# Where the last query projection and the output projection's first part stand among the attention blocks of a two-layer diffusion transformer

## The chip, the cores and the metric

The kernel runs as one program on one core of a Trainium2 chip. The metric is device time of one execution. TensorE (PE, with its weight loads as PEld), VectorE (DVE), ScalarE (ACT), GpSimd (POOL) and SyncE (SP, which here only issues transfers) each work through their own instructions in a fixed order and wait for each other by semaphores.

## The reference, cut to what matters

The network has 2 layers over two streams of 256 tokens: the latents (stream 0) and the context (stream 1). In the last layer only stream 0 goes on past the keys and values. The part between the two feed-forward halves of a layer is the one that is changed:

```python
px = modulate(rms_norm(h, g_mix[l]), sh2, sc2) @ w_in[l]      # and pc for the context
aq, ak, av, hy, nq, nk, nv = split_proj(px)
qa = axial_rope(rms_norm(to_heads(aq, 8), g_q_attn[l]), cos, sin)     # 8 query heads
ya = gqa_latent(qa, ka, av, kca, vca)      # latents see 256 context + 256 latent keys
yb = hyena_mixer(hy, ...)                  # long convolution
yc = neighbourhood_attention(qn, kn, nv, kcn, vcn, rpb)   # 4 heads, with a bias
h = h + gt2 * (jnp.concatenate([ya, yb, yc], -1) @ w_out[l])
# layer 0 only: the same for the context stream, whose queries see the 256 context keys
```

## The kernel before, in words

All of it is in float32. Each dense product is made of three matmuls on split operands: a weight half tile is split into `whi` (ScalarE, line 337) and `wlo` (VectorE, line 338), the activations into `xh` and `xl`. Four split halves can be held at a time.

`mix` (from line 618) runs once per layer. Tokens stand in four blocks `tt` of 128: blocks 2 and 3 are context (256 keys), 0 and 1 latent (512 keys). In layer 0 the order of the blocks is 2, 3, 0, 1, in layer 1 it is 0, 1. There are three groups `g` of four heads: group 0 is the neighbourhood ("near") heads, groups 1 and 2 are the grouped-query heads.

`project(c, use)` (matmuls on lines 680 to 682) is a generator: each step issues 24 matmuls for one stream and half of the weights; after the last step `use` takes the result out of PSUM. With two streams a projection is 4 steps, 96 matmuls, and holds two of the four PSUM banks named `mm`; in layer 1 it is 2 steps, 48 matmuls, one bank. Projection 4 makes the queries of group 1, projection 5 those of group 2. `heads` (lines 695 to 725) normalises and rotates them, `stack_q` (lines 753 to 768) splits and transposes them (line 763) into `qs`.

`attend(tt, g, fill, steps)` (line 836) does one block and group, head by head: scores into an `mm` bank (line 858 for near heads, 863 and 864 for grouped heads), maximum (line 871 or 875), exponential on ScalarE (873 or 877), reciprocal and scaling (878, 879), transposes on TensorE (882), copy to `pT` on ScalarE (884), and after each second head the product with V (889) into an `aux` bank. Between the heads it draws `steps` steps from the generator `fill`, so that other matmuls stand there. Latent near blocks load a bias tile (line 849) into the one buffer `zt`, which the block before has to have read.

Before the change, `fill` in the near group is projections 4 and 5 in a row, 4 steps per block. The first block of group 1 has no filler; then the results of the convolution and of the near heads are split into `xh`, `xl` (chunks 4 to 7; `split`, lines 895 to 897), the queries of group 2 are stacked (they had been kept as `raw` in the list `late`), and from there on `first_part`, the output projection's tiles 0 and 1 over chunks 4 to 7, is the filler: 32 steps of 3 matmuls each (lines 352 to 354), 3 per block in layer 0, 6 in layer 1. What is left of it runs after the last block. The second part, tiles 2 and 3 over chunks 0 to 3, follows.

The order on each engine is set when the program is built: a scheduler works from the order of the Python code with its own estimates, and moves instructions forward or back past each other.

Of the kernel before, what the change touches and what calls it, by code (L numbers as in the profile page):

```python
# [11 lines left out]
F32 = mybir.dt.float32  # L12
# [6 lines left out]
P = 128  # L19
# [3 lines left out]
NT = 512  # L23
# [18 lines left out]
class Net:  # L42
# [575 lines left out]
    def mix(self, l, streams, after):  # L618
        nc, v = self.nc, self.nc.vector
        ns = len(streams)  # L620
        both = (0, 1)
        n = SEQ * ns
        spec, fnorm = self.spec
        with ExitStack() as es:
            mp = es.enter_context(self.tc.tile_pool(name=f"mix{l}", bufs=1))
# [7 lines left out]
            rq = mp.tile([P, 4, 12], F32, name="rq")  # L633
# [4 lines left out]
            for m in range(3):  # L638
                if m < 2:
                    pts = early[m]  # L640
                else:
                    pts = (self.ps(), self.ps())
# [25 lines left out]
            def project(c, use):  # L668
                live = both if c < 2 or c == 3 else streams
                pts = {s: self.ps() for s in live}  # L670
                for half in range(2):
                    hi, lo = self.next_half(("in", l, c), half)
                    for s in live:
                        for i in range(2):
                            t = slice((2 * s + i) * P, (2 * s + i + 1) * P)
                            out = pts[s][:, i * 256:(i + 1) * 256]
                            for k in range(4):
                                kk = half * 4 + k
                                w = slice(k * 256, (k + 1) * 256)
                                nc.tensor.matmul(out, self.xh[:, kk, t], hi[:, w], start=kk == 0 and i == 0, stop=False)  # L680
                                nc.tensor.matmul(out, self.xh[:, kk, t], lo[:, w], start=False, stop=False)  # L681
                                nc.tensor.matmul(out, self.xl[:, kk, t], hi[:, w], start=False, stop=kk == 7 and i == 1)  # L682
                            yield
                use(pts)

            def run(*parts):
                for part in parts:
                    for _ in part:
                        pass

            def heads(src, nh, s, rope, gain, rdst, put):


                w = nh * DH
                raw = mp.tile([P, 2, w], F32, tag="qraw", name="qraw", bufs=4)
                sq = mp.tile([P, 2, w], F32, tag="sqk", name="sqk", bufs=2)
                nc.scalar.copy(raw, src)
                nc.scalar.activation(sq, raw, AF.Square)
                ss = mp.tile([P, 2 * nh], F32, tag="ss", name="ss", bufs=2)
                v.tensor_reduce(out=ss, in_=sq.rearrange("p t (h d) -> p (t h) d", d=DH), axis=AX.X, op=ALU.add)  # L700
                v.tensor_scalar(out=ss, in0=ss, scalar1=1.0 / DH, scalar2=EPS, op0=ALU.mult, op1=ALU.add)
                r = self.rsqrt(ss, 2 * nh, f"q{nh}")
                if rdst is not None:
                    v.tensor_scalar(out=rdst, in0=r.rearrange("p (t h) -> p t h", t=2), scalar1=-0.5 * QSCALE, scalar2=None,
                                    op0=ALU.mult)
                else:
                    r3 = raw.rearrange("p t (h d) -> p (t h) d", d=DH)
                    v.scalar_tensor_tensor(out=r3, in0=r3, scalar=-0.5,
                                           in1=r.rearrange("p (h o) -> p h o", o=1).to_broadcast([P, 2 * nh, DH]),
                                           op0=ALU.mult, op1=ALU.mult)  # L710
                if rope is not None and s == 0:
                    for i in range(2):
                        s5 = sq[:, i].rearrange("p (h a b e) -> p h a b e", h=nh, a=2, b=2)
                        r5 = raw[:, i].rearrange("p (h a b e) -> p h a b e", h=nh, a=2, b=2)
                        st = tabs[:, rope, i, 1].rearrange("p (o a b e) -> p o a b e", o=1, a=2, b=2)
                        for b in range(2):
                            nc.gpsimd.tensor_tensor(out=s5[:, :, :, b], in0=r5[:, :, :, 1 - b],
                                                    in1=st[:, :, :, b].to_broadcast([P, nh, 2, 16]), op=ALU.mult)
                        rh = raw[:, i].rearrange("p (h d) -> p h d", d=DH)
                        v.tensor_tensor(out=rh, in0=rh, in1=tabs[:, rope, i, 0:1, :].to_broadcast([P, nh, DH]), op=ALU.mult)  # L720
                    v.tensor_tensor(out=raw, in0=raw, in1=sq, op=ALU.add)
                else:
                    r3 = raw.rearrange("p t (h d) -> p (t h) d", d=DH)
                    v.tensor_tensor(out=r3, in0=r3, in1=self.gqk[:, l, gain:gain + 1, :].to_broadcast([P, 2 * nh, DH]), op=ALU.mult)
                put(raw, s)
# [26 lines left out]
            def stack_q(p0):  # L752

                def put(raw, s):
                    for t in range(2):
                        st = mp.tile([P, 4, 2, DH], F32R, tag="qraw", name="qst", bufs=4)
                        r = raw[:, t].rearrange("p (h c) -> p h c", h=4)
                        nc.scalar.copy(st[:, :, 0], r)
                        v.tensor_tensor(out=st[:, :, 1], in0=r, in1=st[:, :, 0].bitcast(F32), op=ALU.subtract)
                        pt = self.ps("aux")  # L760
                        flat = st.rearrange("p h w c -> p (h w c)").bitcast(F32)
                        for i in range(4):
                            nc.tensor.transpose(pt[:, i * P:(i + 1) * P], flat[:, i * P:(i + 1) * P], self.ident)
                        tag, bufs = ("uc", 6) if len(qs) < 4 else ("qs", 4)
                        qs[p0, 2 * s + t] = mp.tile([P, 512], F32R, tag=tag, name="qs", bufs=bufs)
                        self.copy(qs[p0, 2 * s + t], pt)
                return put

            two = lambda pt: pt.rearrange("p (t c) -> p t c", t=2)
# [15 lines left out]
                for s in (1, 0):  # L785
                    nc.scalar.copy(V[:, 2 * s:2 * s + 2, P:], two(pts[s]))

            late = []

            def grouped_q(p0):  # L790
                put = stack_q(p0) if p0 == 0 else lambda raw, s: late.append((raw, s))

                def use(pts):
                    for s in streams[::-1]:
                        heads(two(pts[s]), 4, s, 0, 0, rq[:, 2 * s:2 * s + 2, 2 * p0:2 * p0 + 4], put)
                return use

            run(project(0, grouped_kv))
# [3 lines left out]
            zt = mp.tile([P, 2, 512], F32, tag="zt", name="zt")  # L802
# [92 lines left out]
            def split(c0, n, cols, src):  # L895
                nc.scalar.copy(yh[:, c0:c0 + n, cols], src)
                v.tensor_tensor(out=yl[:, c0:c0 + n, cols], in0=src, in1=yh[:, c0:c0 + n, cols].bitcast(F32), op=ALU.subtract)

            order = [0, 1] if ns == 1 else [2, 3, 0, 1]
            fill = chain(project(4, grouped_q(0)), project(5, grouped_q(2)))  # L900
            near = mp.tile([P, 2, NT], F32, name="near")
            for tt in order:
                yo = attend(tt, 0, fill, 4)
                nc.scalar.copy(near[:, :, tt * P:(tt + 1) * P], yo)
            rest = [(g, tt) for g in (1, 2) for tt in order]
            yo = attend(rest[0][1], 1, fill, 0)
            run(fill)
            yh, yl = self.xh, self.xl
            for cb in range(2):
                split(4 + cb, 1, slice(0, n), yt[cb][:, :n].rearrange("p (o t) -> p o t", o=1))  # L910
            split(6, 2, slice(0, n), near[:, :, :n])


            self.begin_sum()
# [12 lines left out]
                                self.residual(pt, l, 5, 4 * m + 2 * half + i, s, s * SEQ)  # L927

            fill = first_part()
            for g, tt in rest:  # L930
                if (g, tt) != rest[0]:
                    yo = attend(tt, g, fill, 3 if ns == 2 else 6)
                if (g, tt) == rest[0]:
                    for raw, s in late:
                        stack_q(2)(raw, s)
                if (g, tt) == rest[-1]:
                    run(fill)
                split(2 * g - 2, 2, slice(tt * P, (tt + 1) * P), yo)
            units = [(m, half) for m in (2, 3) for half in range(2)]
            if ns == 2:  # L940
                hl = {u: self.next_half(("out", l, u[0]), u[1]) for u in units}
                steps = after()
# [148 lines left out]
```

## Time and profile before

| | us |
|---|---|
| median of 3 runs (1768.14 to 1769.57) | 1768.63 |
| the profiled execution's own time | 1769.55 |
| its span in the trace | 1767.8 |
| TensorE busy | 1726.6 |
| VectorE busy | 1146.6 |
| ScalarE busy | 649.3 |

The changed part is two short stretches of the span: attention blocks and fillers run from about 518 to 640 us in layer 0 and from about 1482 to 1551 us in layer 1. Matmuls overlap in their pipeline, so the duration of a row on PE is longer than the step from one matmul to the next; where a row's start is given beside the next one's, the difference is the step. The same holds, by less, for rows on VectorE and ScalarE.

### The profile page before, as it was taken

How to read it: one execution, taken by the hardware profiler on the slowest of the kernel's cores; microseconds unless marked ns; L12 is line 12 of the kernel's file. 1: busy time of each engine (PE TensorE's matmuls, PEld its weight loads, DVE VectorE, ACT ScalarE, POOL GpSimd, SP SyncE). 2: the span in 40 equal slices, each digit the busy share in tenths (PEclk: the TensorE clock that was granted, in tenths of full speed). 3: DMA queues.
4: the chain of work that ended last, by engine and by line, in shares of the span. 5: the costliest groups of instructions: out<-in, count | busy, mean ns of one | idle time of the engine just before them, and what ended most of it. 6: DMA issues, size and time to landing. Idle time of an engine off the chain costs nothing.

```text
span 1767.8 us, 24967 instructions
## 1 busy us (share of the span) xinstructions
PE 1726.6 (98%) x9996; PEld 1478.5 (84%) x9996; DVE 1146.6 (65%) x2218; ACT 649.3 (37%) x1053; POOL 90.5 (5%) x128
## 2 busy tenths in 40 slices
PE   7999999999999999999999999999999999989999
PEld 3787888889887688888888898888888898789999
DVE  4778778757657868676676475454544587865554
ACT  4422222234337744222222342222222355744443
POOL 0000000011110020000000110000000301010000
PEclk9999999999999999999999999999999999989999
DMA  7765455532211023544543335534432233135553
GB/s 266 294 194 179 178 183 204 181 124 72 96 60 37 25 85 132 172 163 168 164 177 141 110 110 190 172 126 147 160 134 87 93 130 110 49 119 171 182 185 131
DMA packets 47429, 251.95 MB, mean 143 GB/s; under 512 B 5999, under 2 KB 7233, under 8 KB 29521
## 3 DMA queue, kind: packets, MB, share of 16 engines
q1 hardware_dynamic: 47106, 250.26, 40.9%
q8 instruction: 78, 1.28, 0.3%
q14 instruction: 37, 0.30, 0.1%
q0 software_dynamic: 64, 0.10, 0.0%
q10 hardware_dynamic: 144, 0.01, 0.0%
HBM read 249.30 MB, written 1.05 MB: 142 GB/s over the span
## 4 chain that ended last, share of the span: by engine, by line
PE 90%; DVE 6%; ACT 2%; issue 1%; POOL 0%; DMA 0%; DVEq 0%; POOLq 0%; ACTq 0%
PE mm L352 26%; PE mm L353 26%; PE mm L354 25%; PE mm L680 2%; PE mm L682 2%; PE mm L681 2%; PE aux L889 1%; DVE wlo L338 1%; PE aux L882 1%; ACT whi L337 1%; PE aux L613 1%; PE mm L858 1%; PE aux L827 1%; DVE h L447 0%; PE aux L125 0%
## 5 line engine op out<-in xcount | busy, mean ns | idle before, releaser
L352 PE MATMUL mm<-xh,whi 128*128 128x512 f32 (+1 forms) x1760 | 607.7, 349 | 9.0 <-ACT xh L441 3.8
L353 PE MATMUL mm<-xl,whi 128*128 128x512 f32 (+1 forms) x1760 | 609.6, 348 | 3.2 <-DVE xl L442 2.0
L354 PE MATMUL mm<-xh,wlo 128*128 128x512 f32 (+1 forms) x1760 | 608.6, 347 | 0.0
L338 DVE TENSOR_TENSOR wlo<-raw,whi 128x1024 fp32r<-128x1024 f32 x324 | 387.3, 1197 | 233.0 <-ACT whi L337 229.5
L337 ACT CAST whi<-raw 128x1024 fp32r<-128x1024 f32 x324 | 332.3, 1027 | 541.5 <-PE mm L353 353.7
L352 PEld LDWEIGHTS mm<-xh,whi 128*128 128x128 f32 x1760 | 332.1, 190 | 55.5 <-ACT xh L201 6.4
L353 PEld LDWEIGHTS mm<-xl,whi 128*128 128x128 f32 x1760 | 334.4, 190 | 47.0 <-DVE xl L442 2.6
L354 PEld LDWEIGHTS mm<-xh,wlo 128*128 128x128 f32 x1760 | 333.9, 190 | 42.2 <-issue 2.2
L352 PE MATMUL mm<-hh,whi 128*128 128x512 f32 (+1 forms) x788 | 271.2, 344 | 0.0
L353 PE MATMUL mm<-hl,whi 128*128 128x512 f32 (+1 forms) x788 | 271.0, 344 | 0.1
L354 PE MATMUL mm<-hh,wlo 128*128 128x512 f32 (+1 forms) x788 | 270.3, 343 | 0.0
L505 DVE TENSOR_TENSOR gs<-gs,mm 128x512 f32<-128x512 f32 (+1 forms) x88 | 54.5, 621 | 186.1 <-ACT gs L504 147.7
L352 PEld LDWEIGHTS mm<-hh,whi 128*128 128x128 f32 x788 | 149.3, 189 | 19.2 <-issue 1.9
L353 PEld LDWEIGHTS mm<-hl,whi 128*128 128x128 f32 x788 | 149.3, 190 | 18.9 <-issue 1.1
L354 PEld LDWEIGHTS mm<-hh,wlo 128*128 128x128 f32 x788 | 149.3, 189 | 17.4
L447 DVE SCALAR_TENSOR_TENSOR h<-mm,mod,h 128x256 f32<-128x256 f32 x216 | 98.6, 479 | 90.9 <-PE mm L354 90.2
L285 DVE CUSTOM_DVE_ANT_0 ada<-ada,cb 128x1024 f32<-128x1024 f32 x128 | 155.9, 1221 | 2.4 <-DMA ada<-wada 0.4
L504 ACT ACTIVATE gs<-mm 128x512 f32<-128x512 f32 (+1 forms) x88 | 47.8, 544 | 275.6 <-PE mm L354 271.7
L285 DVE CUSTOM_DVE_ANT_0 prod<-ada,cb 128x1024 f32<-128x1024 f32 x96 | 116.9, 1218 | 0.0
L374 POOL TENSOR_TENSOR acc<-acc,sq 128x256 f32<-128x256 f32 x61 | 52.7, 869 | 1234.7 <-ACT sq L370 1195.9
L680 PE MATMUL mm<-whi,xh 128*128 128x256 f32 x336 | 97.4, 290 | 0.0
L681 PE MATMUL mm<-wlo,xh 128*128 128x256 f32 x336 | 96.7, 288 | 0.0
(178 smaller groups left out, 1443.5 us busy)
## 6 DMA issues: line engine op xcount, KB each, us to landing
raw<-wgu SPq DMA_DIRECT2D x86, 1024.0 KB, 4.8
ada<-wada SPq DMA_DIRECT2D x128, 512.0 KB, 3.7
raw<-wd SPq DMA_DIRECT2D x32, 896.0 KB, 4.6
raw<-wd SPq DMA_DIRECT2D x16, 1024.0 KB, 4.9
raw<-win SPq DMA_DIRECT2D x12, 1024.0 KB, 4.8
a<-wada SPq DMA_DIRECT2D x8, 1024.0 KB, 5.2
raw<-wout SPq DMA_DIRECT2D x8, 1024.0 KB, 4.9
raw<-why SPq DMA_DIRECT2D x6, 1024.0 KB, 4.9
```

The costliest lines, as they stand in the source:

```text
L285: nc.vector.tensor_tensor_reduce(out=prod, in0=w, in1=self.cb[:, s], scale=1.0, scalar=0.0, op0=ALU.mult, op1=ALU.add, accum_out=m[:, s, j ...
L337: nc.scalar.copy(hi[:, :n], raw)
L338: nc.vector.tensor_tensor(out=lo[:, :n], in0=raw, in1=hi[:, :n].bitcast(F32), op=ALU.subtract)
L352: t.matmul(out, whi, xhi, start=start, stop=False)
L353: t.matmul(out, whi, xlo, start=False, stop=False)
L354: t.matmul(out, wlo, xhi, start=False, stop=stop)
L374: nc.gpsimd.tensor_tensor(out=self.acc[s], in0=self.acc[s], in1=sq, op=ALU.add)
L447: return self.nc.vector.scalar_tensor_tensor(out=self.h[:, j, cols], in0=ps[:, c0:c0 + SEQ], scalar=self.mod(l, ch, s, j), in1=self.h[:, j ...
L504: nc.scalar.activation(gs[:, :n], pg[:, :n], AF.Silu)
L505: nc.vector.tensor_tensor(out=gs[:, :n], in0=gs[:, :n], in1=pu[:, :n], op=ALU.mult)
L680: nc.tensor.matmul(out, self.xh[:, kk, t], hi[:, w], start=kk == 0 and i == 0, stop=False)
L681: nc.tensor.matmul(out, self.xh[:, kk, t], lo[:, w], start=False, stop=False)
```

## The change

Projection 4 alone is now the filler of the near group, and projection 5 becomes that of group 1. The output of group 1 isn't split block by block: ScalarE copies each block from PSUM into a new buffer `first` (which takes the buffer `zt`), and one split of all blocks follows. `first_part` now stands wholly in group 2. The list `late` is gone: the queries of group 2 are stacked as soon as they are made. In Python the numbers of steps are also set anew.

```diff
             def grouped_q(p0):
-                put = stack_q(p0) if p0 == 0 else lambda raw, s: late.append((raw, s))
-
                 def use(pts):
                     for s in streams[::-1]:
-                        heads(..., rq[:, 2 * s:2 * s + 2, 2 * p0:2 * p0 + 4], put)
+                        heads(..., rq[:, 2 * s:2 * s + 2, 2 * p0:2 * p0 + 4], stack_q(p0))
                 return use
...
-            fill = chain(project(4, grouped_q(0)), project(5, grouped_q(2)))
+            pace = (3, 3, 2, 1) if ns == 2 else (3, 2)
             near = mp.tile([P, 2, NT], F32, name="near")
-            for tt in order:
-                yo = attend(tt, 0, fill, 4)
+            fill = project(4, grouped_q(0))
+            for tt, steps in zip(order, pace):
+                yo = attend(tt, 0, fill, steps)
                 nc.scalar.copy(near[:, :, tt * P:(tt + 1) * P], yo)
-            rest = [(g, tt) for g in (1, 2) for tt in order]
-            yo = attend(rest[0][1], 1, fill, 0)
+            run(fill)
+            fill = project(5, grouped_q(2))
+            first = mp.tile([P, 2, NT], F32, tag="zt", name="first")
+            for tt, steps in zip(order, pace):
+                yo = attend(tt, 1, fill, steps)
+                nc.scalar.copy(first[:, :, tt * P:(tt + 1) * P], yo)
             run(fill)
...
             split(6, 2, slice(0, n), near[:, :, :n])
+            split(0, 2, slice(0, n), first[:, :, :n])
...
             fill = first_part()
-            for g, tt in rest:
-                if (g, tt) != rest[0]:
-                    yo = attend(tt, g, fill, 3 if ns == 2 else 6)
-                if (g, tt) == rest[0]:
-                    for raw, s in late:
-                        stack_q(2)(raw, s)
-                if (g, tt) == rest[-1]:
+            for tt, steps in zip(order, (2, 6, 12, 12) if ns == 2 else (10, 22)):
+                yo = attend(tt, 2, fill, steps)
+                if tt == order[-1]:
                     run(fill)
-                split(2 * g - 2, 2, slice(tt * P, (tt + 1) * P), yo)
+                split(2, 2, slice(tt * P, (tt + 1) * P), yo)
```

First place: TensorE in layer 0, in the last near block (`kT,qT` are near scores, `ident,pr` transposes, `pT,V` products with V, `whi,xh` and its like a projection). Before, its last scores stand among matmuls of projection 5:

```order
L858 MATMUL mm<-kT,qT 128x512
L882 MATMUL aux<-ident,pr 128x128 x4
L681 MATMUL mm<-wlo,xh 128x256
L858 MATMUL mm<-kT,qT 128x512
L682 MATMUL mm<-whi,xl 128x256
L680 MATMUL mm<-whi,xh 128x256
L681 MATMUL mm<-wlo,xh 128x256
```

After, from the block's first score to the first score of group 1 (`khi,qs`), with `ident,qst` as the transposes of group 1's queries:

```order
L682 MATMUL mm<-whi,xl 128x256
L854 MATMUL mm<-kT,qT 128x512
L878 MATMUL aux<-ident,pr 128x128 x8
L854 MATMUL mm<-kT,qT 128x512 x2
L885 MATMUL aux<-pT,V 64x128 x8
L854 MATMUL mm<-kT,qT 128x512
L878 MATMUL aux<-ident,pr 128x128 x8
L885 MATMUL aux<-pT,V 64x128 x8
L878 MATMUL aux<-ident,pr 128x128 x8
L763 MATMUL aux<-ident,qst 128x128 x7
L885 MATMUL aux<-pT,V 64x128 x8
L763 MATMUL aux<-ident,qst 128x128
```

No filler is left between the last near block's first score and group 1's first score.

Second place: TensorE in layer 0, in the last latent block of group 1. Before, matmuls of `first_part` stand among its heads:

```order
L863 MATMUL mm<-khi,qs 128x512
L889 MATMUL aux<-pT,V 64x128 x8
L864 MATMUL mm<-klo,qs 128x512
L352 MATMUL mm<-xh,whi 128x512
L353 MATMUL mm<-xl,whi 128x512
L882 MATMUL aux<-ident,pr 128x128 x4
L354 MATMUL mm<-xh,wlo 128x512
```

After, from the last matmul of projection 5 on:

```order
L682 MATMUL mm<-whi,xl 128x256
L859 MATMUL mm<-khi,qs 128x512
L885 MATMUL aux<-pT,V 64x128 x8
L878 MATMUL aux<-ident,pr 128x128 x8
L860 MATMUL mm<-klo,qs 128x512
L859 MATMUL mm<-khi,qs 128x512
L860 MATMUL mm<-klo,qs 128x512
L859 MATMUL mm<-khi,qs 128x512
L885 MATMUL aux<-pT,V 64x128 x8
L860 MATMUL mm<-klo,qs 128x512
```

The scores of the last head, two batches of transposes, two products with V and the transposes of group 2's queries follow, without a filler, until group 2 begins; the 96 matmuls of `first_part` then stand among group 2's heads, 87 of them before its last score.

## Rows read from the trace of the kernel before

**Rows 1.** The page: span and busy time by engine.
```profile
span 1767.8 us, 24967 instructions
PE 1726.6 (98%) x9996; PEld 1478.5 (84%) x9996; DVE 1146.6 (65%) x2218; ACT 649.3 (37%) x1053; POOL 90.5 (5%) x128
```

**Rows 2.** Windows: stretch, its length, busy time by engine, TensorE clock, DMA.
```profile
518.00:567.00 49.00, 48.54 (x350) 37.21 (x349) 33.59 (x113) 31.71 (x75) 1.91 (x4) 1.00 0.15 55
567.00:601.00 34.00, 29.66 (x219) 21.82 (x217) 28.80 (x105) 25.84 (x64) 2.31 (x4) 0.95 0.10 32
601.00:640.00 39.00, 38.28 (x288) 29.52 (x287) 28.47 (x89) 24.43 (x62) 0.00 (x0) 1.00 0.20 67
1482.00:1507.00 25.00, 23.85 (x177) 18.39 (x177) 20.82 (x58) 19.76 (x40) 1.89 (x4) 1.00 0.29 106
1507.00:1529.00 22.00, 20.09 (x179) 16.23 (x179) 21.14 (x69) 18.58 (x43) 2.01 (x4) 1.00 0.14 50
...
580.00:590.00 10.00, 7.38 (x37) 5.11 (x37) 8.49 (x32) 5.87 (x16) 0.00 (x0) 0.83 0.32 107
660.00:670.00 10.00, 6.98 (x53) 6.32 (x52) 9.49 (x23) 5.62 (x11) 4.46 (x4) 1.00 0.29 105
```

**Rows 3.** Timeline of PE, 566 to 590 us: the rows with idle time before them.
```profile
572.52 0.66 PE L889 MATMUL aux<-pT,V 128*64 128x128 f32 x8 [0.48 <-ACT pT L884]
...
574.95 0.41 PE L882 MATMUL aux<-ident,pr 128*128 128x128 f32 x2 [0.88 <-DVE rst L72]
...
582.93 0.38 PE L863 MATMUL mm<-khi,qs 128*128 128x256 f32 x1 [1.29 <-ACT pr L877]
...
584.34 0.50 PE L863 MATMUL mm<-khi,qs 128*128 128x512 f32 x1 [0.91 <-ACT pr L877]
```

**Rows 4.** Timeline of PE: steps of fillers, near scores, products with V, transposes.
```profile
512.02 0.28 PE L680 MATMUL mm<-whi,xh 128*128 128x256 f32 x1
512.14 0.28 PE L681 MATMUL mm<-wlo,xh 128*128 128x256 f32 x1
...
539.50 1.13 PE L858 MATMUL mm<-kT,qT 64*128 64x512 f32 x4
...
561.21 1.12 PE L858 MATMUL mm<-kT,qT 64*128 64x512 f32 x2
...
562.93 1.09 PE L889 MATMUL aux<-pT,V 128*64 128x128 f32 x16
...
568.26 1.09 PE L882 MATMUL aux<-ident,pr 128*128 128x128 f32 x8
...
637.06 0.39 PE L352 MATMUL mm<-xh,whi 128*128 128x512 f32 x1
637.29 0.39 PE L353 MATMUL mm<-xl,whi 128*128 128x512 f32 x1
```

**Rows 5.** Timeline of DVE in a latent near block.
```profile
541.17 1.22 DVE L338 TENSOR_TENSOR wlo<-raw,whi 128x1024 fp32r<-128x1024 f32 x1 [4.24 <-ACT whi L337]
542.31 0.48 DVE L870 SCALAR_TENSOR_TENSOR pr<-mm,rq,bias 128x256 f32<-128x256 f32 x1
542.71 0.67 DVE L700 TENSOR_REDUCE ss<-sqk 128x8 f32<-128x512 f32 x1
543.30 0.67 DVE L871 TENSOR_REDUCE mx<-pr 128x1 f32<-128x512 f32 x1
...
546.64 0.47 DVE L879 TENSOR_SCALAR pr<-pr,mx 128x512 f32<-128x512 f32 x1
547.04 0.16 DVE L73 TENSOR_SCALAR rsu<-rst 128x8 f32<-128x8 f32 x1
```

**Rows 6.** Groups of ACT by line and shape, 518 to 640 us.
```profile
L884 ACT COPY pT<-aux 128x512 f32<-128x512 f32 x24 | 13.9, 588 | 5.8 <-PE aux L882 5.2
...
L877 ACT ACTIVATE pr<-mm,mx,rq 128x512 f32<-128x512 f32 x16 | 12.4, 781 | 2.4 <-DVE mx L876 2.4
```

**Rows 7.** The bias tile: its landing time.
```profile
DMA to landing us min/median/max: 3.3/3.4/3.6
```

More of the change, by code (lines that the diff above doesn't have):

```diff
@@ L786, in near_v @@
                     nc.scalar.copy(V[:, 2 * s:2 * s + 2, P:], two(pts[s]))
-            late = []
             def grouped_q(p0):
-                put = stack_q(p0) if p0 == 0 else lambda raw, s: late.append((raw, s))
                 def use(pts):
                     for s in streams[::-1]:
-                        heads(two(pts[s]), 4, s, 0, 0, rq[:, 2 * s:2 * s + 2, 2 * p0:2 * p0 + 4], put)
+                        heads(two(pts[s]), 4, s, 0, 0, rq[:, 2 * s:2 * s + 2, 2 * p0:2 * p0 + 4], stack_q(p0))
                 return use
```

## The prediction, written before the changed kernel was run

> **What bounds the kernel now.** I read the page first: TensorE is busy for 1726.6 of 1767.8 us, VectorE and ScalarE for far less [rows 1]. The change neither adds nor removes a matmul: projections 4 and 5, the 96 matmuls of `first_part` per layer, scores, transposes and products with V are all still there. So the time can only move by what TensorE waits, by its clock, and by whether neighbouring instructions overlap. Then I cut the two attention stretches into stages [rows 2]. In layer 0 the near group (518 to 567 us) leaves TensorE almost no idle time, 49.00 - 48.54 = 0.5 us, though VectorE is busy for only 33.6 of 49 us: projections 4 and 5 fill everything. Group 1 (567 to 601) leaves it 34.00 - 29.66 = 4.3 us, at a clock of 0.95. Group 2 (601 to 640) leaves 0.7 us. The timeline puts the idle time of group 1 in its first 18 us, where its first block has no filler: 0.48, 0.88, 1.29 and 0.91 us are the larger waits [rows 3]; the clock in 580 to 590 is 0.83 [rows 2]. In layer 1 the idle time is 25.00 - 23.85 = 1.15 us in the near group and 22.00 - 20.09 = 1.9 us in group 1, with VectorE busy for 20.8 of 25 and 21.1 of 22 us [rows 2].
>
> So there is little to win: 4.3 + 1.15 + 1.9 = 7.4 us of idle time and the clock. The question is where TensorE waits after the change, because the same fillers are spread over the same heads in another way.
>
> **What goes.** (a) Layer 0, the first block of group 1 now has projection 5 beside it: its 4.3 us go. The low clock goes with them: 0.05 x 34 us = 1.7 us at full use, and TensorE is busy for 87% of that stretch, so 1.5 us. (b) Layer 1: 1.15 + 1.9 = 3.1 us; I count them all as gone, since every wait there gets other neighbours, and count the new waits below. (c) Near scores of two heads lie on different halves of the array and overlap when they stand next to each other: two take 1.13 us (539.50), one alone 1.12 us (561.21) [rows 4]. Before, of the 8 latent near heads of layer 0, one pair stands together and six scores alone, after the change two pairs and four alone: 1.05 us less. In layer 1 it is three pairs and two alone before, four pairs after: another 1.05 us. Sum of what goes: 4.3 + 1.5 + 3.1 + 2.1 = 11.0 us.
>
> **What comes, layer 0, near group.** Its two latent blocks now have only the last 36 matmuls of projection 4, and none at all in the second block. Take the stretch from the first latent score to the first score of group 1. TensorE's work, in steps of rows 4: 36 fillers at 0.12 = 4.3; scores 2 pairs and 4 alone, 6 x 1.05 = 6.3; 32 transposes, four times eight at about 1.0 = 4.0; four products with V at 1.03 = 4.1; the transposes of the first stream's queries 1.0; sum 19.7 us. VectorE's work in the same stretch, in steps from one start to the next [rows 5]: per head 0.40 (scale and bias), 0.60 (maximum), 0.40 (scaling) and two short ones, 0.10 together: 1.5, times 8 heads = 12.0. Beside that, before the last head is scaled, 1.5 for the reduction, gain and short ones of projection 4's context heads, and one weight split, 1.14. The second block's bias can be fetched only when the first block's last read is done, and lands 3.4 us later [rows 7]; about half of it is covered by the first block's own exponentials and scaling: 1.7. In front 1.1 for the first score, behind 2.5 for the last transposes (0.5), two copies (0.5 each) and product (1.0), and some twenty hand-overs between engines that I put at 0.1 each, an estimate: 2.1. Sum 22.0, so TensorE waits for 22.0 - 19.7 = 2.3 us. Bounds: below 0 it can't go; above, the stretch of now that is bare in the same way costs 4.3 + 1.5 = 5.8.
>
> **Layer 0, end of group 1.** From the first latent score of group 1 on, TensorE has 24 fillers (2.9), 16 score matmuls at 0.23 (3.7), transposes 4.0, products 4.1 and query transposes 1.0: 15.7 us. Here ScalarE is later than VectorE: it has 8 exponentials at 0.78 (12.4 over 16) and 8 copies at 0.58 (13.9 over 24) [rows 6], 10.9, or 10.1 with their overlap of 0.1 each; besides, before the last copy, the casts of the convolution's and the near heads' results (1.1 and 1.05), two copies to `first` (0.6), the raw copies and squares of projection 5 (2.1), two casts of the queries (0.7), and one weight cast (1.0), together 6.6; in these sizes, which are by elements those of the copies of rows 6, 16.7 in all. With 0.5 in front, 1.0 for the last product and 0.9 of hand-overs: 19.1. TensorE waits for 3.4 us. Same bounds, 0 and 5.8.
>
> **Banks and starts.** While a projection runs with two streams, only two `mm` banks are left for scores, and the next score has to wait for an exponential. Before, 24 fillers (2.9 us) stood between two pairs of near scores, now 12 (1.4 us): I put 1.2 us at the near group's second pair, 1.0 in group 1's first block, and 1.0 at the first block of group 2, whose exponentials stand behind the second stream's query work on VectorE. Together 3.2, between 0 (the scheduler's other rows cover it) and 5.
>
> **Layer 1.** Each projection is 48 matmuls here. Near group: TensorE 5.8 + 4.2 (four pairs) + 4.0 + 4.1 + 1.0 = 19.1; VectorE 12.0 + one stream's query work 4.2 (0.6 each for reduction, sum and cast, 0.7 + 0.7 for rotation and split, 1.0 short ones) + three weight splits 3.4 + 1.1 in front + 2.0 behind = 22.7: 3.6 us of waiting. Group 1: TensorE 5.8 + 3.7 + 4.0 + 4.1 + 1.0 = 18.6, VectorE 8 x 1.1 = 8.8 + 4.2 + 1.9 (splits) + 1.1 (weight split) + 3.0 in front and behind = 19.0: 0.4. Together 4.0, bounds 0 and twice the 5.8 of above.
>
> What costs nothing: the copies to `first` (six 128x256 copies on ScalarE) beyond those counted, since group 2 is bound by TensorE, 38.3 of 39 us [rows 2], and now has more fillers than before; and the missing tail, because the second part's matmuls over chunks 0 and 1 are ready and cover the last split. SyncE's queue keeps its order of weights; the bias of the second block moves ahead of one weight tile.
>
> **Sum.** What comes: 2.3 + 3.4 + 3.2 + 4.0 = 12.9. Less the 11.0: +1.9 us. On the profiled execution, 1769.55 (span 1767.8 and 1.75 around it), that is 1771.5; that execution is 0.9 above the median, so on the median 1768.63 + 1.9 = 1770.5. A measurement of this kernel can tell about 0.2%, 3.5 us, from no change: the forecast is no change that can be told.
>
> **A page beside it.** After the waits of rows 3 the clock reads 0.83 in 580 to 590, a part of it at 1.2 GHz; in 660 to 670, with TensorE busy for only 7.0 of 10 us, it stays at 1.00 [rows 2]. The Trainium skill, TensorE: Matmul & The Clock Gate (Part 1), says that the throttled state is the default and activity releases it. By that rule alone each of the four bare stretches could fall to the lower clock, and the sum would be +1.9 + 4 x 1.7 = +8.7; the second row speaks against it, the first for it. It is part of the second rival.
>
> **Rivals.** (1) Faster: the bare stretches pack as densely as layer 1's near group does now, 1.15 us idle in 25 [rows 2]. Four times 1.15 = 4.6 and 1.0 for banks is 5.6 against 11.0: -5.4, 1763.2. For it: VectorE is at 20.8 of 25 there without holding TensorE up. Against: 96 fillers stood there, now 48. It decides from the point where all new waits together are under 7.5 us. (2) Slower: a bare stretch at the end of a group behaves like the bare stretch of now, scores that wait for exponentials and then the low clock, 5.8 us. In layer 0 twice, 11.6, with 3.2 for banks and layer 1 as above 4.0, is 18.8 - 11.0 = +7.8, 1776.4; in all four, 23.2 + 3.2 - 11.0 = +15.4, 1784.0. For it: both bare stretches end with a product that waits for the last copy, and the queries of the next group stand in the same queues. Against: the stretch of now carries two streams of queries and three splits on VectorE at once, 9 us of work; the new ones carry one and the start of the other. It decides from 14.5 us of new waits. (3) The change does not do what it says, because the scheduler pulls the fillers back: the order shows them where the code puts them, 0.02, at 1768.6.
>
> **Chances.** Forecast 0.40, with its own range 1767 to 1772; rival 1 0.20; rival 2 0.38; rival 3 0.02. That gives faster 0.20, same 0.41 (the forecast's tail and rival 3 within it), slower 0.39. The range 1762 to 1780 takes in rival 1 and the first form of rival 2.
>
> **What would show it.** TensorE's idle time between the end of projection 4 and group 1's first score (2 to 3 us) and between the end of projection 5 and group 2's first score (3 to 4 us) in layer 0; no idle time in the first block of group 1; clock rows at 1.00 in both. The forecast is wrong if these two sum to over 9 us, or to under 2, and a step of it fails where VectorE or ScalarE shows gaps of its own there.

## The result, and the profile after

The change makes the kernel slower: 1788.42 us median (1785.63 to 1789.53) against 1769.10 us for the kernel before, ratio 1.0109 (95% interval 1.0097 to 1.0121). The forecast was 1770.5 us with a range of 1762 to 1780. The profiled execution took 1787.99 us, its span is 1786.1 us. Its page begins:

```profile
span 1786.1 us, 24963 instructions
...
PE 1732.8 (97%) x9996; PEld 1484.3 (83%) x9996; DVE 1154.2 (65%) x2214; ACT 652.2 (37%) x1055; POOL 90.8 (5%) x128
```

Beside [rows 1] these two rows split the loss. TensorE has the same 9996 matmuls as before and is busy for 6.2 us longer with them; the clock in the rows below is the likely reason for most of it. And it is idle for 1786.1 - 1732.8 = 53.3 us instead of 41.2, 12.1 us more. Together that is the whole 18.3 us of span. The windows say where (stretch, its length, busy time of PE, PEld, DVE, ACT and POOL, TensorE clock, DMA share, GB/s); they answer to [rows 2]:

```profile
518.00:536.00 18.00, 18.00 (x131) 14.07 (x130) 10.06 (x34) 11.33 (x28) 0.00 (x0) 1.00 0.17 59
536.00:551.00 15.00, 14.65 (x100) 8.83 (x98) 10.15 (x25) 11.00 (x25) 0.00 (x0) 1.00 0.17 45
551.00:563.00 12.00, 8.56 (x59) 6.83 (x59) 9.55 (x37) 7.45 (x18) 0.52 (x2) 0.72 0.18 76
563.00:579.00 16.00, 15.46 (x136) 14.18 (x135) 12.30 (x49) 10.46 (x30) 1.45 (x3) 1.00 0.01 2
...
589.00:601.00 12.00, 9.20 (x77) 7.07 (x75) 10.29 (x32) 10.28 (x22) 0.00 (x0) 0.86 0.14 38
601.00:645.00 44.00, 41.59 (x270) 31.99 (x265) 34.04 (x108) 25.18 (x59) 1.92 (x4) 1.00 0.10 38
1489.00:1505.00 16.00, 15.98 (x112) 11.03 (x112) 11.47 (x28) 12.00 (x25) 0.00 (x0) 1.00 0.29 100
1505.00:1518.00 13.00, 7.77 (x60) 5.63 (x56) 10.79 (x34) 8.47 (x21) 3.06 (x4) 0.87 0.24 81
1518.00:1532.00 14.00, 13.87 (x115) 12.14 (x116) 10.23 (x28) 9.75 (x22) 0.00 (x0) 1.00 0.00 1
1532.00:1546.00 14.00, 8.16 (x58) 5.92 (x56) 10.44 (x31) 8.14 (x16) 2.06 (x4) 0.76 0.23 77
1546.00:1570.00 24.00, 23.95 (x210) 21.24 (x208) 18.10 (x46) 15.08 (x29) 0.00 (x0) 1.00 0.13 44
```

Every group begins full and ends empty. The four ends (551 to 563, 589 to 601, 1505 to 1518, 1532 to 1546) hold 3.44, 2.80, 5.23 and 5.84 us of idle time, and the clock is below 1.00 in these four and in no other row. Group 1's first two blocks (563 to 579) keep 0.54 us; before, the longer waits of [rows 3] stood there and directly behind. In an end no engine is busy all the time, VectorE for 10.79 of 13 us: TensorE waits for a chain that goes from engine to engine. The timeline of PE in the near group's end of layer 1 shows it (start, duration, engine, line, operation, out<-in, number of instructions, then in brackets the idle time before it and what released it):

```profile
1506.66 1.33 PE L878 MATMUL aux<-ident,pr 128*128 128x128 f32 x8 [1.14 <-DVE pr L875]
1508.96 1.09 PE L885 MATMUL aux<-pT,V 128*64 128x128 f32 x16 [0.98 <-ACT pT L880]
1512.28 1.22 PE L878 MATMUL aux<-ident,pr 128*128 128x128 f32 x8 [2.22 <-DVE pr L875]
```

(Lines are 4 lower than before from the projections' users on: 878 is the transpose, 885 the product with V, 875 the scaling, 880 the copy.) Two heads are scaled, transposed, copied, multiplied; then the next two. Their product, at 1514.23, runs at the lower clock: 1.98 us instead of 1.09. Why the second pair comes so late stands in ScalarE's rows of the same stretch, and in VectorE's:

```profile
1503.84 0.37 ACT L901 COPY near<-aux 128x256 f32<-128x256 f32 x1 [1.20 <-PE aux L885]
1504.49 0.58 ACT L697 COPY qraw<-mm 128x512 f32<-128x512 f32 x1 [0.28 <-PE mm L682]
1504.98 0.72 ACT L869 ACTIVATE pr<-pr,mx 128x512 f32<-128x512 f32 x1
...
1508.80 1.06 ACT L337 CAST whi<-raw 128x1024 fp32r<-128x1024 f32 x1
1509.75 0.73 ACT L869 ACTIVATE pr<-pr,mx 128x512 f32<-128x512 f32 x1
```

```profile
1505.82 0.17 DVE L874 RECIPROCAL mx<-mx 128x1 f32<-128x1 f32 x1 [2.35 <-ACT pr L869]
...
1509.89 1.22 DVE L338 TENSOR_TENSOR wlo<-raw,whi 128x1024 fp32r<-128x1024 f32 x1
...
1511.44 1.28 DVE L875 TENSOR_SCALAR pr<-pr,mx 128x512 f32<-128x512 f32 x2
```

An exponential (L869) stands behind two copies that wait for TensorE, and the next one behind a weight's cast; VectorE is idle for 2.35 us, then has a weight split ahead of the scaling. And nothing else is left for TensorE: projection 4 ends at 1504.5, and its queries, which go through the same two queues, come behind the near group's last product (L885). PE's rows after, and the same of before (L763 the queries' transposes, L859 and L863 a score of group 1, L889 the product):

```profile
1514.23 1.98 PE L885 MATMUL aux<-pT,V 128*64 128x128 f32 x16 [0.73 <-ACT pT L880]
1516.14 1.77 PE L763 MATMUL aux<-ident,qst 128*128 128x128 f32 x8
1518.04 0.50 PE L859 MATMUL mm<-khi,qs 128*128 128x512 f32 x1
```

```profile
1503.65 1.06 PE L763 MATMUL aux<-ident,qst 128*128 128x128 f32 x8 [0.37 <-DVE rsu L74]
...
1507.17 0.40 PE L863 MATMUL mm<-khi,qs 128*128 128x512 f32 x1
...
1513.65 1.09 PE L889 MATMUL aux<-pT,V 128*64 128x128 f32 x16
```

Before, group 1 begins 6.5 us ahead of the near group's last product; after, 3.8 us behind it. So the starts of two stages are no measure of the work between them: the groups overlapped.

### The profile page after: what moved, and what is told of

Its sections match the earlier page's. It is cut to its first block, busy times and chain, and to the rows that moved or that the text cites. A ratio compares the mean times of both kernels' runs of the same rounds, so it can differ in the third digit from the quotient of the medians.

```text
span 1786.1 us, 24963 instructions
## 1 busy us (share of the span) xinstructions
PE 1732.8 (97%) x9996; PEld 1484.3 (83%) x9996; DVE 1154.2 (65%) x2214; ACT 652.2 (37%) x1055; POOL 90.8 (5%) x128
## 3 DMA queue, kind: packets, MB, share of 16 engines
q8 instruction: 79, 1.29, 0.3%
## 4 chain that ended last, share of the span: by engine, by line
PE 91%; DVE 5%; ACT 2%; issue 1%; POOL 0%; DMA 0%; DVEq 0%; ACTq 0%; POOLq 0%
PE mm L352 26%; PE mm L353 26%; PE mm L354 25%; PE mm L680 2%; PE aux L885 2%; PE mm L682 2%; PE mm L681 2%; PE aux L878 2%; DVE wlo L338 1%; PE mm L854 1%; PE aux L613 1%; PE aux L823 1%; PE mm L859 0%; PE mm L860 0%; ACT whi L337 0%
```

## The experiments

**One layer at a time.** Kernel 1 has the changed order in layer 0 alone, kernel 2 in layer 1 alone (`if ns == 2:` or `if ns == 1:` the changed code, `else:` the code of before).

> The changed order in layer 0 (two streams), the order of before in layer 1. The two traces put the start of layer 1's attention 6.7 us later after the change, of which 5.4 lie in layer 0's attention, and the rest of the loss in layer 1. Theory A (every bare end of a group costs by itself what the traces show in it): 1769.1 + 5.4 to 6.7 = 1774.5 to 1775.8 us. Rival B (layer 1 loses because of what layer 0 passes on, such as weights that come later): about the whole loss, 1788. Rival C (the profiled execution misleads about the layers): layer 0 loses half, 1778 to 1779.

> The order of before in layer 0, the changed order in layer 1 (one stream). Theory A: the rest of the loss, 13 us from 1769.1: 1781 to 1783 us, with lower clock in the two bare stretches of layer 1. Rival B (layer 1 loses through layer 0): no loss, 1769 to 1771. Rival C: half, 1778 to 1779.

Measured 1775.59 us, ratio 1.0037 [1.0025, 1.0050], and 1781.63, ratio 1.0069 [1.0055, 1.0083]. The two losses add: +6.9 and +13.0, each against the kernel before, beside +19.3 for both. Rivals B and C fall; layer 1 loses by itself, and twice as much.

**Idle products in the ends.**

```diff
+    for _ in range(idle):
+        nc.tensor.matmul(yo[:, 256:], khi[:, 0, 256:384], khi[:, 1, 256:512], start=True, stop=True)
```

> The changed kernel, with six idle products of 256 columns (0.12 us each, 0.7 us) behind each head of the last block of the near group and of group 1, into the unused half of that block's output bank: 48 in each layer, 11.5 us of additional work on TensorE in all, of which nothing is used. Theory A with the clock as a large part of the loss: the four falls of the clock in the bare stretches go (20.5 us at 1.2 GHz in the profile after), the softmax chain stays as long as it is: 1780 to 1785 us, faster than the 1788.4 of the changed kernel though more is computed. Theory A with the chain alone (waits of TensorE for VectorE and ScalarE, the clock a mere sign): the products fall into idle time, 1787 to 1790. Rival D (TensorE's own work bounds these stretches, and the waits are of no account): they add their time, 1797 to 1800.

Measured 1792.32 us, ratio 1.0129 [1.0115, 1.0142]: between the cases, a miss for all three. The page of this kernel:

```profile
span 1791.8 us, 25157 instructions
...
PE 1744.2 (97%) x10092; PEld 1496.3 (84%) x10092; DVE 1155.0 (64%) x2214; ACT 651.9 (36%) x1055; POOL 91.8 (5%) x128
```

TensorE is busy for 11.4 us more and idle for 5.7 us less than after the change. So half of the added work fell into waits, and the span grew by the rest. The clock fell all the same in three of the four ends (0.96 over layer 0's near group and group 1, 0.94 over layer 1's, after 0.94 and 0.91). In the near group's end of layer 1 it stayed up:

```profile
1508.00:1523.00 15.00, 11.31 (x98) 9.26 (x97) 12.11 (x37) 9.45 (x21) 2.80 (x4) 1.00 0.19 72
```

From the first near score to group 1's first score it is 28.6 us there, with 24 idle products in it, after 29.2. In this one end, then, most of the length is the chain and not the clock. What the clock costs over all four, this kernel does not tell.

**No block without fillers.** Kernel 4: `chain(project(4, ...), project(5, ...))` drawn at three steps a block through the near group and half of group 1, `first_part` from there on.

> Another distribution of the same work: projections 4 and 5 run on from one into the other over the near group and the first half of group 1's blocks (three steps a block), only that half's results wait in a buffer, and the output projection's first part begins in the second half of group 1. No block is bare of fillers. Theory A (a loss wherever a block has no filler beside its softmax chain): the loss of the change goes, and the waits of group 1's first block before the change (4.3 us and the clock) too: 1763 to 1768 us. Rival E (it is the additional work in the queues of ScalarE and VectorE, the buffer's copies and splits and the early stacking of projection 5's queries, that costs): most of it is here too, 1778 to 1786.

Measured 1773.47 us, ratio 1.0025 [1.0016, 1.0035]. Fifteen of the 19 us are back, but the kernel before is not beaten: theory A's range (1763 to 1768) and rival E's (1778 to 1786) are both missed. In layer 0 one wait is left, and it holds nearly all the idle time there:

```profile
589.36 0.79 PE L859 MATMUL mm<-khi,qs 128*128 128x512 f32 x1 [4.77 <-ACT pr L873]
```

The windows of that kernel show who is busy meanwhile, VectorE for 10.65 of 11 us:

```profile
578.00:589.00 11.00, 6.03 (x35) 4.28 (x34) 10.65 (x36) 7.48 (x18) 2.03 (x4) 1.00 0.00 1
```

Its rows in this stretch are two streams of query work, the splits of three results (L893), and only then the small operation (L872) on which the exponential, and so the score's bank, depends:

```profile
581.44 1.22 DVE L893 TENSOR_TENSOR xl<-near,xh 128x1024 fp32r<-128x1024 f32 x1
...
587.11 0.69 DVE L721 TENSOR_TENSOR qraw<-qraw,sqk 128x512 f32<-128x512 f32 x1
...
587.79 0.15 DVE L872 SCALAR_TENSOR_TENSOR mx<-mx,rq 128x1 f32<-128x1 f32 x1
```

The kernel before has the same picture at the same point, where projection 5 ends. So rival E is not the cause of most of the loss, but a narrower form of it, theory E below, may be the cause of this wait. The next two kernels test that.

**Query work later.** Kernel 5 is kernel 4 in layer 0 and the kernel before in layer 1; kernel 10 is the kernel before. In both, layer 0 only copies projection 5's results out of the banks where it ends; the rest follows behind group 1's last two blocks. Kernel 5 also splits the buffered half of group 1 only in group 2. The cut shows the copies (in both) and the rest (as kernel 10 has it):

```diff
+    if p0 and ns == 2:
+        for s in streams[::-1]:
+            held[s] = mp.tile([P, 2, 4 * DH], F32, tag="qraw", name="qraw", bufs=4)
+            nc.scalar.copy(held[s], two(pts[s]))
+        return
...
+    if ns == 2 and g == 1 and tt < 2:
+        heads(None, 4, 1 - tt, 0, 0, rq[:, 2 - 2 * tt:4 - 2 * tt, 4:8], stack_q(2), held[1 - tt])
```

> Layer 1 as before the change. Layer 0 as in the kernel with the fillers over the edges, with two things taken out of the place where its only long wait stood (4.9 us at 584 to 589, a score that waits while VectorE does two streams of query work, the splits of three results and a weight split, 578 to 588): projection 5's results are only copied out there, their norm, rotation and stacking follow one stream each behind group 1's last two blocks, and the buffered half of group 1 is split only in group 2. Theory E (waits come where query work and splits of a whole projection meet the softmax chain in the queues of VectorE and ScalarE): the 4.9 us and the low clock behind it (1.7) go, layer 0 ends 5 to 6 us earlier than before the change: 1762 to 1765 us. Theory A (the loss is that of heads without fillers): there are none in either, so the wait only moves: 1767 to 1771.

> The kernel before the change, with one edit in layer 0: where projection 5 ends (group 1's first block), its results are only copied out of the banks; norm, rotation and stacking follow behind group 1's third and fourth block, one stream each. Theory E (queue work meets the softmax chain): the 4.3 us of waits in that block and the low clock (1.5) go, 1763 to 1766 us. Theory A (that block waits because it has no fillers; it still has none): 1768 to 1770.

Measured 1763.52 us, ratio 0.9970 [0.9959, 0.9982], and 1764.93, ratio 0.9978 [0.9968, 0.9988]: theory E is twice within its range, and both kernels are faster than the one before the change. In kernel 5's group 1 the wait and the lower clock are gone, and so they are in kernel 10's (second row):

```profile
560.30:595.80 35.50, 35.09 (x270) 27.89 (x270) 30.86 (x99) 28.19 (x69) 2.15 (x4) 1.00 0.09 31
565.20:592.50 27.30, 26.82 (x213) 20.81 (x212) 24.53 (x91) 24.28 (x61) 0.00 (x0) 1.00 0.11 40
```

Kernel 10's first block of group 1 still has no projection beside it. So what [rows 3] show was not a block that lacked fillers, as the prediction had it, but a softmax chain behind query work. The timeline of before says so too. The last head of the first block is scored and the first filler of the first part stands there at

```profile
569.43 0.28 PE L863 MATMUL mm<-khi,qs 128*128 128x256 f32 x1
...
573.11 0.50 PE L352 MATMUL mm<-xh,whi 128*128 128x512 f32 x1
```

Of the four waits only the one of 0.48 us comes before that filler. Those of 1.29 and 0.91 us stand at 582.93 and 584.34, ahead of the second block's last head and the third block's first.

**The queries' path, and where the fillers stand.** Kernel 6 leaves the norm and the rotation of the grouped queries out; kernels 7 and 8 change the pace (after: 3, 3, 2, 1 and 3, 2).

> The changed kernel without the norm and the rotation of the grouped queries: the copy out of the bank is stacked as it is (left out: squares, reduction, root, gain, rotation and its GpSimd part, two layers, two projections). Theory Q (the path from the last product of a projection to the next group's first score, which needs its queries at once, sets the end of the bare stretches: 13.5 us from 1504.5 to 1518.0 in layer 1): most of the loss goes, 1772 to 1778 us. Theory A (the softmax chain of bare heads): 1783 to 1787, only the work that stood between.

> The changed kernel with the same projections drawn earlier in their group: steps 5, 4, 0, 0 over the four blocks in layer 0 (3, 3, 2, 1 after the change) and 5, 0 in layer 1 (3, 2). The last block is wholly bare, the queries are ready earlier. Theory A: more bare heads, 24 matmuls (2.9 us) less beside them in layer 0 and 12 (1.4 us) in layer 1, each twice: up to 8.6 us more, 1790 to 1797 us. Theory Q: the query path begins some 5 us earlier and no longer ends the group: 1778 to 1784.

> The opposite: 2, 2, 2, 3 in layer 0 and 2, 3 in layer 1. Theory A: the last block has fillers behind three of its four heads, less waiting there: 1780 to 1785 us. Theory Q: the projection ends later, its queries too, and the next group's first score waits for them with nothing beside: 1790 to 1796.

Measured 1783.04 us, ratio 1.0081 [1.0067, 1.0095]; 1790.71, ratio 1.0127 [1.0113, 1.0140]; 1791.04, ratio 1.0128 [1.0115, 1.0142]. Without norm and rotation 5.4 of the 19.3 us come back, as theory A has it, so these are a minor part here. Moving the fillers does not help either way: kernel 7 falls in theory A's range, kernel 8 in theory Q's. The stretch from the first near score to group 2's first score in layer 1, after and in kernels 7 and 8, in that order:

```profile
1488.80:1545.70 56.90, 45.67 (x338) 34.65 (x337) 42.63 (x119) 38.15 (x81) 5.12 (x8) 0.91 0.19 66
```

```profile
1494.40:1543.30 48.90, 39.78 (x297) 31.39 (x297) 38.53 (x115) 34.95 (x74) 3.95 (x8) 0.93 0.17 55
```

```profile
1489.90:1548.10 58.20, 45.93 (x337) 35.51 (x336) 43.11 (x119) 37.81 (x81) 3.93 (x8) 0.88 0.18 64
```

The stretch of kernel 7 is shorter, but it holds fewer matmuls (297), because group 2 begins there (1543.31) before group 1's last copy to `first` (1550.62). A better measure is the time from the keys of layer 1 (their first transposes, line 747) to the end of the span: 332.6 us after, 328.2 in kernel 7, 333.9 in kernel 8. Early queries gain 4.3 us there, though a whole block is bare (theory Q); late ones, with fillers beside more heads, lose 1.3 (against A). Up to these keys it is 1453.5 us after, 1459.1 in kernel 7 and 1454.6 in kernel 8: in layer 0 the bare blocks of kernel 7 cost 5.5 us, more than it gains in layer 1. Neither theory explains both layers; each had one half of the cause.

**Both halves apart.** Kernel 9 has a bare near end in layer 1, but queries that are ready by then: projection 4 runs ahead of the near heads, projection 5 beside them, and the first part beside groups 1 and 2. Its layer 0 is as before. Kernel 11 has late queries but the fillers of before. The cuts are against the changed kernel (kernel 9, layer 1) and against the one before (kernel 11).

```diff
+run(project(4, grouped_q(0)))
+fill = project(5, grouped_q(2))
-fill = project(4, grouped_q(0))
```

```diff
+put = lambda raw, s: (late if p0 else early).append((raw, s))
-put = stack_q(p0) if p0 == 0 else lambda raw, s: late.append((raw, s))
...
+for raw, s in early:
+    stack_q(0)(raw, s)
 rest = [(g, tt) for g in (1, 2) for tt in order]
```

> Layer 0 as before the change. Layer 1: projection 4 runs whole ahead of the near group, and projection 5 takes its place beside the near heads, step for step as projection 4 stood there after the change; the first part of the output projection runs beside groups 1 and 2. The near group has the same fillers and the same bare heads as after the change; only the queries of group 1 are ready before it ends. Theory D (the loss is a drain: a group whose queries come from a projection beside the group ahead of it can't begin until that group has ended, so the softmax chain empties and fills again): the near stage, from its first score to group 1's first score, is 21 to 24 us instead of 29.2, and the time 1768 to 1773. Theory A (bare heads): near stage 28 to 30 us, time 1775 to 1779.

> The kernel before the change, with all its fillers where they are, but the stacking of group 1's queries (split, transposes, copies) put behind the near group's last block instead of directly behind projection 4. Theory D (drain): group 1's first score waits for the near group's end, as after the change; the near stage of layer 1 grows from 25.0 to 28 to 31 us, that of layer 0 from 48.5 to 50 to 52, and the time to 1774 to 1780. Theory A (bare heads; nothing is barer than before): 1767 to 1771.

Measured 1772.49 us, ratio 1.0020 [1.0011, 1.0029], and 1770.05, ratio 1.0008 [0.9999, 1.0017]. Kernel 9's near stage fell from 29.2 to 18.4 us, more than D expected, and its time stands in D's range. But in kernel 11 the near stage of layer 1 grew from 25.0 to 29.3 us, as D said, and the time did not follow (D missed, A's 1767 to 1771 met); the next stage was that much shorter. The drain alone costs nothing that these runs can tell. From the first near score to group 2's first score in layer 1, before, kernel 9 and kernel 11 (after is the first of the three rows above):

```profile
1482.16:1525.17 43.01, 40.14 (x320) 31.64 (x320) 38.33 (x116) 34.86 (x74) 3.90 (x8) 1.00 0.24 87
```

```profile
1487.40:1531.10 43.70, 39.51 (x298) 29.51 (x297) 38.58 (x118) 33.32 (x73) 3.78 (x8) 1.00 0.21 76
```

```profile
1482.10:1524.90 42.80, 39.63 (x312) 30.58 (x311) 37.62 (x115) 34.57 (x74) 3.61 (x8) 1.00 0.26 87
```

Idle are 2.9, 4.2 and 3.2 us, and 11.2 after. But these four stretches differ behind the near group as well: group 1 has the first part beside it in all of them but after. So the near group has to be read alone, from its first score to the end of its last product with V. Before (queries ready, fillers), kernel 9 (ready, bare), kernel 11 (late, fillers) and after (late, bare):

```profile
1482.16:1514.74 32.58, 30.56 (x233) 23.30 (x233) 28.40 (x80) 27.02 (x56) 1.89 (x4) 1.00 0.29 103
1487.45:1517.63 30.18, 26.30 (x188) 18.07 (x188) 27.38 (x88) 23.04 (x50) 3.78 (x8) 1.00 0.21 75
1482.10:1511.44 29.34, 27.36 (x218) 21.07 (x217) 24.61 (x67) 24.19 (x49) 1.90 (x4) 1.00 0.28 91
1488.82:1516.21 27.39, 22.23 (x162) 15.38 (x162) 21.52 (x60) 20.12 (x42) 3.06 (x4) 0.96 0.28 97
```

Idle are 2.0, 3.9, 2.0 and 5.2 us, and only the last has a low clock. From the keys of layer 1 to the end the four take 320.9, 324.0, 319.9 and 332.6 us. TensorE has two covers for the softmax chain, a projection's matmuls and the next group's heads. At the near group's end the fillers alone keep all of the time; ready queries alone keep the clock and leave part of the waits. The change takes both away at the same place.

Two reservations. Of the 3.1 us that kernel 9 loses in layer 1, 1.1 are idle time and 2.0 busy time; two of its pairs of near scores take 2.38 and 1.74 us where a pair takes 1.13, and a few matmuls of the first part also moved into its near end. And the other 6.1 us of after's idle time lie behind the near group's last product, most of them in group 1's end, where kernels 9 and 11 have both covers. Which of the two is needed there is not shown.

**The clock by itself.** Kernel 12 is kernel 5 with six idle products between the mean and the spread of the norm behind layer 1's attention.

> The fastest kernel so far (1763.5 us: fillers over the edges and late query work in layer 0) with six idle products in the longest wait that is left, the norm behind layer 1's attention (TensorE idle for 2.6 us at 1560, then 6.83 us at 1.2 GHz from 1561.4); nothing uses them. It asks for the price of the clock by itself: no wait gets shorter. If the lower clock costs what it takes from matmuls that stand dense, half of the 6.83 us goes: 1760 to 1761.5 us, and no low clock in 1560 to 1572. If it stands beside waits that would be there anyway, the low clock goes and the time stays, 1763 to 1764. If 2.6 us of products don't hold the clock: 1763 to 1764.5 with the low clock still there.

Measured 1763.33 us, ratio 0.9970 [0.9958, 0.9982], the time of kernel 5. The same 7 us in kernel 5 and in kernel 12, and in kernel 12 the 4.2 us of the idle products alone:

```profile
1561.00:1568.00 7.00, 4.22 (x18) 3.96 (x19) 5.20 (x18) 1.87 (x4) 0.00 (x0) 0.53 0.33 136
```

```profile
1559.10:1563.30 4.20, 4.20 (x15) 3.43 (x15) 2.28 (x13) 0.00 (x0) 0.00 (x0) 0.64 0.73 250
1561.00:1568.00 7.00, 5.88 (x33) 5.16 (x33) 4.36 (x14) 1.87 (x4) 0.00 (x0) 0.81 0.29 121
```

About half of the low clock went (over 1555 to 1575 the granted clock is 0.83 in kernel 5 and 0.91 in kernel 12), and no time with it. The clock fell while TensorE was busy with the idle products (4.20 of 4.20 us, 0.64); they then took 4.37 us instead of the 2.6 foreseen, and the spread stood behind them: its first matmul is at 1563.28, in kernel 5 at 1562.66. The price of the clock stays open here.

## Why the prediction was wrong

The sum was +1.9; measured were +19.3 in the medians and 18.3 in the two spans. Of the 16.4 us that the sum lacks in the spans, 6.6 are idle time (5.5 more forecast, 12.1 measured) and 9.8 busy time (3.6 less forecast, 6.2 more measured).

- **What goes** went: group 1's first two blocks in layer 0 have no wait over 0.5 us and a clock of 1.00, though the reason given for the old waits was wrong (kernel 10). Layer 1's 3.1 us can't be told apart from what came there. Of the 2.1 us for near pairs layer 0's half came: two pairs and four alone. Layer 1's did not: three pairs, at 1.13, 1.78 and 1.13 us, and two alone, no more pairs than before.
- **Layer 0's waits** came out right in sum, in part by luck. Near end 2.3 forecast, 3.44 measured; group 1's end 3.4 and 2.80; banks and starts 3.2, and 0.54 + 2.41 in the two rows behind the ends. That is 8.9 against 9.2. But each wait was a difference of two sums, and all of these were too small: from the first latent score to group 1's first score it is 26.4 us with TensorE busy for 22.6 (22.0 and 19.7 forecast), in group 1 22.3 and 19.5 (19.1 and 15.7). The 0.1 us for a hand-over came from no row; in the near end of layer 1 a copy ends 0.04 us before the product that needs it (1508.34 + 0.58 and 1508.96), a scaling 0.15 us before its transposes (1506.02 + 0.49 and 1506.66).
- **Layer 1's waits** are the first term that failed: 4.0 forecast, 5.23 + 5.84 = 11.1 measured; the 7.1 us between them are more than the 6.6 that are missing in all. For the near group I took TensorE's 19.1 us and VectorE's 22.7 us as running beside each other over the whole group. Both sums were too small: VectorE was busy for 11.47 + 10.79 = 22.3 us (of the 22.7, 19.6 were its own work), TensorE for 15.98 + 7.77 = 23.75, part of it at the lower clock. But either fits into 29 us, and the stage has two phases: 16.0 us in which TensorE is full and VectorE has time to spare, then 13.0 us in which the chain sets the pace. They add up: 29 us. The larger of two sums holds only where either engine's work can be done at any time within the stage. Group 1 is the same, 0.4 forecast, 5.84 measured; there VectorE's work was too small as well, 16.0 (8.8 + 4.2 + 1.9 + 1.1) against 10.23 + 10.44 = 20.7.
- **The clock** is the second: I kept it at 1.00 in the new ends, and it fell in all four. TensorE's busy time grew by 6.2 us, where 3.6 less was forecast (1.5 and 2.1). Priced as the prediction priced it (one minus the clock, times the busy time of the row), the four ends cost 2.4 + 1.3 + 1.0 + 2.0 = 6.7 us and group 1 before 1.5: an estimate of 5.2 of the 6.2. The Trainium skill, TensorE: Matmul & The Clock Gate (Part 1), has the throttled state as the default that activity releases. The four ends agree with that (0.72, 0.86, 0.87, 0.76). The row that I held against the lower clock, 660 to 670 [rows 2], with 3 us idle and a clock of 1.00, did not bear on these ends.
- **The second rival** came nearest with its form for all four ends (1784.0). Its price of 5.8 us an end was of the right size: with the estimate above, idle time and clock make 5.8, 4.1, 6.2 and 7.8 us. But it took that price from a stretch whose cause was another, the query work that kernels 5 and 10 removed.
- **What the working lacked** is that the queries of the next group were ready early before the change: group 1's scores stood beside the last near heads, 1507.17 and 1513.65 in the rows above. The prediction counted fillers per stage and did not ask what else TensorE could have done. The four kernels with and without either cover show this for the near group of layer 1; for group 1's end it is argued from them.

The section on the kernel before counts 24 matmuls a step; a step is 12, eight of them in layer 0 and four in layer 1. The prediction's sums go by matmuls and do not change.

## What to carry to other kernels

Before moving a filler, ask at each place where it leaves what else the engine could run there; here a chain was fully exposed only where both the fillers and the next independent work were missing, and moving one thing took both. Add phases, not stages: where an engine is full first and waits later, the times add, even if each engine's sum is below the stage's length. A wait named after an exponential may be query work ahead of a small operation in VectorE's queue: deferring that work, not filling the wait, made this kernel 0.2 to 0.3% faster than before.

## What the runs showed of the hardware

- The lower clock came in all four new ends (0.72 to 0.87), while 660 to 670 before the change, with 3 us idle, kept 1.00 [rows 2]. It also came over idle products that left TensorE no gap (0.64 in kernel 12), behind small matmuls with waits of 0.42 and 0.53 us. With such products in the ends, kernel 3 kept 1.00 in one of the four.
- Two scalings on VectorE took 1.28 us together beside GpSimd's rotation in the near group's end of layer 1, and 0.49 us each before it began. No run isolates this.
